# Weight-block sums of two seven-product multiplications: from VectorE and a table in HBM to accumulating DMAs at load time

## The chip, the core and the metric

The kernel runs on one NeuronCore of a Trainium2 chip. Its work is spread over TensorE (PE, with its weight loads PEld), VectorE (DVE), ScalarE (ACT), GpSimd (POOL) and the queue that issues most DMAs (SP). The metric is the device time of one execution in microseconds; lower is better.

## The reference, cut to what matters

The program is one block of a streaming encoder, in float32, for 16 meta tokens and 1024 frames of width 1024: a token mixer with four mLSTM heads and four retention heads, an output projection with a residual, and a gated MLP with a causal convolution, a down projection and a residual.

```
h = h + token_mixer(rmsnorm(h, norm_mix_g), ...)        # ends in: (mixed @ w_out)
h = h + channel_mixer(rmsnorm(h, norm_ffn_g), ...)
    a = causal_dwconv(u @ w_up, ffn_conv_w)
    (silu(a) * (u @ w_gate)) @ w_down
return rmsnorm(h, norm_final_g)
```

`w_out` is 2048 x 1024 and `w_down` 2816 x 1024. The change concerns these two products alone.

## The kernel before, in words

Every float32 matmul is made of three: both operands are split into a high and a low part (`hi`, rounded by ACT, and `lo`, the rest by DVE), and hi·hi, hi·lo and lo·hi are added up in PSUM.

The time runs in stages: the eight heads (token mixer), the output product `w`, the up and gate products, the down product `d`. In the mixers each head has its o projection beside its scan, then the next head's v projection, then its q and k projections (`qk_group`, three pieces of the tokens each).

The output and the down product are computed by seven block products instead of eight (class `Seven`, objects `mixw` and `down`). The weight matrix is cut in 2 x 2 blocks: w11 and w21 are the two column halves of the upper rows, w12 and w22 those of the lower rows. The activations are cut in two row halves and two token halves, A1, A2, B1, B2. Products "1", "2" and "4" each use a plain weight block. The pairs "65" and "73" use two sums of blocks each, in one 128 x 1024 tile per step. A product goes over `kn` row blocks of 128 (8 for `w`, 11 for `d`); the steps (stage, k) stand in the order 1, 65, 73, 4, 2 for `w` and 1, 2, 65, 73, 4 for `d`. A step of "65" or "73" issues 24 matmuls of 128x512, into the PSUM banks `pwx`, `pwy` (or `pdx`, `pdy`), which `give` adds to the residual when a stage has ended.

Each step has three parts. `load` brings the weight tile from HBM by a DMA on SP, into a ring: the tiles `raw_w` (two, of the general ring `raw`) and then `wdh` and `wdl` (two halves each) for `w`, four `rd` tiles for `d`. `prep` splits it (CAST on ACT into `hi_w` or `hi_d`, TENSOR_TENSOR on DVE into `lo_w` or `lo_d`; three such pairs in a ring), and splits the activations (`rsplit`). `mms` issues the matmuls. A tile of the load ring is free again when its `lo` has been made; the load for the step four uses later waits for that. `wdh` and `wdl` lie in memory that the mixers' pool `mix` gives back; the first load into them waits for the last instruction that uses that pool, and among those users are the activation tiles `wtk` and `wtq` of step 65, k=0.

The weight sums of "65" and "73" are made long before, in the mixers: `wsum(g, k)` is called three times per head, after pieces of the q and k projections of heads 1 to 7, until its 19 calls are done (8 for `w_out`, 11 for `w_down`). A call loads two 128 x 1024 row blocks (tiles named `wsw` or `wsd`), makes four additions on DVE and stores four 128 x 512 results in HBM tensors, also named `wsw` and `wsd`. `load` of the later stages then reads one 512 KB tile of these.

A scheduler that the framework brings sets the order of instructions on each engine; the engines run their queues in that order and wait on semaphores. A DMA waits on the queue that issues it, and holds up what stands behind it there.

Of the kernel before, what the change touches and what calls it, by code (L numbers as in the profile page):

```python
# [17 lines left out]
P = 128  # L18
# [12 lines left out]
HB = 4 * P  # L31
# [30 lines left out]
def body(ctx, tc, h_in, vecs, cst, mask_in, rot, w_v0, w_v, w_fm, w_out, w_up, w_gate, w_down, out):  # L62
# [121 lines left out]
    sums = {(g, st, k): dram.tile([P, 2 * HB], F32, name=f"ws{g}{st}_{k}") for g, n in (("w", 8), ("d", KD)) for st in ("65", "73") for k in range(n)}  # L184

    def wsum(g, k):
        src, n = (w_out, 8) if g == "w" else (w_down, KD)
        a, b = (accp.tile([P, 2 * HB], F32, tag=f"rr{i}", name=f"ws{g}{k}_{i}") for i in range(2))
# [3 lines left out]
        after(nc.vector.tensor_tensor(w22, w21, w22, ALU.add), last["qk"])  # L192
        nc.vector.tensor_tensor(w21, w21, w11, ALU.subtract)
# [5 lines left out]
    wsums = [(g, k) for g, n in (("w", 8), ("d", KD)) for k in range(n)]  # L199

    def u_m(h):
        for b in range(2):
# [352 lines left out]
            m.append(nc.tensor.matmul(pt, al, xh_, start=False, stop=last and k == n - 1, skip_group_check=True))  # L555
        return m[0], m[-1]

    def rsplit(x, tiles, late=False):
        hi, lo = (t[:, :x.shape[1]] for t in tiles)
        m = nc.scalar.copy(hi, x), V.tensor_tensor(lo, x, hi.bitcast(F32), ALU.subtract)  # L560
        if late:
            behind(m)
        else:
            last["rsplit"] = m
        return hi, lo
# [9 lines left out]
    class Seven:  # L575
# [10 lines left out]
        def load(self, t):  # L586
# [5 lines left out]
            if st in self.QUARTER:  # L592
                kb, mb = self.QUARTER[st]
                if k % 2 == 0:
                    n = min(2, self.kn - k)
                    x = self.raw(st, nm)
                    nc.sync.dma_start(x[:, :HB * n].rearrange("p (k j) -> p k j", j=HB),
                                      self.wd[k + kb * self.kn:k + kb * self.kn + n, :, mb * HB:(mb + 1) * HB].rearrange("k p j -> p k j"))
                    r["w"] = x[:, :HB * n]
            else:  # L600
                x = self.raw(st, nm)
                nc.sync.dma_start(x[:, :2 * HB], sums[self.nm, st, k])
                r["l"] = x[:, :2 * HB]
            self.draws[t] = r

        def pre4(self, t):
# [23 lines left out]
        def prep(self, t):  # L630
# [17 lines left out]
            elif st in self.QUARTER:  # L648
                if k % 2 == 0:
                    self.w = fsplit(nm, [d["w"]])  # L650
                r = rsplit(act[{"1": "A1", "2": "A2", "4": "A1"}[st], k], self.rt(st, k, 0))
                self.ops[t] = [(half_of(self.w, k % 2), r, "xy"[st == "2"])]
            elif st == "65":
                a1, a2, b2 = (act[q, k] for q in ("A1", "A2", "B2"))
# [6 lines left out]
            else:  # L661
                w = fsplit(nm, [d["l"]])
                r7 = rsplit(act["B1", k], self.rt(st, k, 0))
                r3 = rsplit(act["B2", k], self.rt(st, k, 1))
                self.ops[t] = [(half_of(w, 1), r7, "x"), (half_of(w, 0), r3, "y")]
            self.read(t)

# [322 lines left out]
    for h in range(8):  # L990
# [595 lines left out]
```

## Time and profile before

| what | value |
|---|---|
| median of 3 runs | 1552.53 us (1551.2 to 1552.64) |
| profiled execution, its span | 1551.5 us; its own time is not given apart from the span |
| busy: PE, PEld, DVE, ACT, POOL | 1518.8, 1395.5, 1124.2, 737.2, 2.4 us |
| bytes moved by DMA | 197.41 MB, 127 GB/s on average |
| HBM written | 49.32 MB |

The span is the time from the first to the last instruction; it lies 1.0 us below the median of the runs. A row of a view names the line in the kernel, the engine, the operation, what is written and read, the shapes, the count and the durations. SP's own waiting and issuing is written SPq. The view by stretches gives the busy time of each engine in a piece of the span, then the granted clock of TensorE (PEclk), the busy share of the 16 DMA engines, and GB/s. Tile names in the profile carry no numbers, so that all four halves of the ring read `wdh` or `wdl`.

### The profile page before, as it was taken

Reading aid. Unit: us, or ns where it says so; the run is one execution under the profiler, and the core shown is the slowest. Engines: PE = TensorE matmul, PEld = TensorE weight load, DVE = VectorE, ACT = ScalarE, POOL = GpSimd, SP = SyncE. Lnnn points to the kernel's source line nnn. Section 1 sums busy time; section 2 is a strip of 40 time slices with the busy share of each in tenths; the row PEclk is TensorE's granted clock in tenths of the full one; section 3 lists DMA queues with packets and bytes.
Section 4 is the critical chain, followed back from the end, with each engine's and each line's share of the span. In section 5 each row is a group of like instructions: output and inputs, shape, how many; then the busy total and the mean of one; then the engine's idle time right before and its main releaser. Section 6 shows DMA issues by size and latency. Waiting matters only on the chain.

```text
span 1551.5 us, 25426 instructions
## 1 busy us (share of the span) xinstructions
PE 1518.8 (98%) x9763; PEld 1395.5 (90%) x9763; DVE 1124.2 (72%) x2388; ACT 737.2 (48%) x1493; POOL 2.4 (0%) x12
## 2 busy tenths in 40 slices
PE   8999999999999999999999999999999999999997
PEld 8989999999989999998788998999999999888887
DVE  8757768696767767678867778666666666778657
ACT  7574655455243343436454455444444444434443
POOL 0000000000000000000000000000000000000000
PEclk9999999999999999999999999999999999999999
DMA  6125435263533525226542326332222224923313
GB/s 219 36 70 163 152 110 188 79 218 97 181 122 126 167 85 189 94 91 245 177 139 100 101 78 195 96 102 89 82 80 78 82 82 137 385 96 116 95 42 109
DMA packets 92441, 197.41 MB, mean 127 GB/s; under 512 B 9048, under 2 KB 31264, under 8 KB 92320
## 3 DMA queue, kind: packets, MB, share of 16 engines
q1 hardware_dynamic: 92176, 195.73, 38.2%
q8 instruction: 76, 1.25, 0.3%
q14 instruction: 45, 0.37, 0.1%
q10 hardware_dynamic: 144, 0.07, 0.0%
HBM read 146.44 MB, written 49.32 MB: 126 GB/s over the span
## 4 chain that ended last, share of the span: by engine, by line
PE 87%; DMA 5%; DVE 4%; ACT 2%; issue 1%; SPq 0%; DVEq 0%; ACTq 0%
PE pv L373 4%; PE pv L374 4%; PE pv L375 3%; PE po L385 3%; PE po L384 3%; PE po L383 3%; PE pdx L553 3%; PE pdx L555 3%; PE pdx L554 3%; PE pup_x L554 2%; PE pup_x L555 2%; PE pga_x L553 2%; PE pga_x L555 2%; PE pga_x L554 2%; PE pup_x L553 2%; DMA A<-scr 2%
## 5 line engine op out<-in xcount | busy, mean ns | idle before, releaser
L373 PE MATMUL pv<-hi_v,uh 128*128 128x256 f32 (+1 forms) x512 | 147.1, 288 | 6.1 <-DVE vl L349 1.9
L374 PE MATMUL pv<-lo_v,uh 128*128 128x256 f32 (+1 forms) x512 | 146.6, 287 | 0.0
L375 PE MATMUL pv<-hi_v,ul 128*128 128x256 f32 (+1 forms) x512 | 146.0, 286 | 0.0
L383 PE MATMUL po<-uh,hi_o 128*128 128x386 f32 (+2 forms) x384 | 125.7, 327 | 0.0
L384 PE MATMUL po<-ul,hi_o 128*128 128x386 f32 (+2 forms) x384 | 123.9, 323 | 0.0
L385 PE MATMUL po<-uh,lo_o 128*128 128x386 f32 (+2 forms) x384 | 123.6, 322 | 0.0
L373 PEld LDWEIGHTS pv<-hi_v,uh 128*128 128x128 f32 x512 | 97.8, 191 | 10.1 <-issue 2.9
L374 PEld LDWEIGHTS pv<-lo_v,uh 128*128 128x128 f32 x512 | 97.7, 191 | 0.6 <-DVE lo_v L150 0.5
L375 PEld LDWEIGHTS pv<-hi_v,ul 128*128 128x128 f32 x512 | 97.7, 191 | 0.1
L242 ACT CAST hi_up<-raw_up 128x512 fp32r<-128x512 f32 (+1 forms) x52 | 36.5, 719 | 108.2 <-PE pga_z L554 61.0
L383 PEld LDWEIGHTS po<-uh,hi_o 128*128 128x128 f32 x384 | 72.9, 190 | 0.2
L384 PEld LDWEIGHTS po<-ul,hi_o 128*128 128x128 f32 x384 | 72.8, 190 | 0.2
L385 PEld LDWEIGHTS po<-uh,lo_o 128*128 128x128 f32 x384 | 72.7, 189 | 0.1
L243 DVE TENSOR_TENSOR lo_ga<-fraw_ga,hi_ga 128x512 fp32r<-128x512 f32 (+1 forms) x52 | 41.8, 807 | 36.9 <-ACT hi_ga L242 36.8
L553 PE MATMUL pup_x<-uh_g,hi_up 128*128 128x256 f32 (+1 forms) x240 | 67.2, 282 | 1.2 <-ACT uh_g L1021 1.2
L554 PE MATMUL pup_x<-ul_g,hi_up 128*128 128x256 f32 (+1 forms) x240 | 67.4, 283 | 0.1
L243 DVE TENSOR_TENSOR lo_up<-raw_up,hi_up 128x512 fp32r<-128x512 f32 (+1 forms) x52 | 41.2, 809 | 35.1 <-ACT hi_up L242 34.3
L383 PE MATMUL pq<-uh,hi_q 128*128 128x400 f32 (+2 forms) x192 | 63.2, 329 | 3.1 <-DVE vl L349 1.9
L555 PE MATMUL pup_x<-uh_g,lo_up 128*128 128x256 f32 (+1 forms) x240 | 66.2, 282 | 0.0
L383 PE MATMUL pk<-uh,hi_k 128*128 128x400 f32 (+2 forms) x192 | 62.3, 324 | 0.5 <-DVE rq L404 0.5
L243 DVE TENSOR_TENSOR lo_d<-rd,hi_d 128x1024 fp32r<-128x1024 f32 (+1 forms) x34 | 37.7, 1112 | 34.0 <-ACT hi_d L242 34.0
L384 PE MATMUL pq<-ul,hi_q 128*128 128x400 f32 (+2 forms) x192 | 62.1, 324 | 0.0
(747 smaller groups left out, 4981.4 us busy)
## 6 DMA issues: line engine op xcount, KB each, us to landing
wsd<-w_down_d SPq DMA_DIRECT2D x22, 512.0 KB, 4.1
wsd<-wsd SPq DMA_DIRECT2D x44, 256.0 KB, 2.5
raw_up<-w_up_d SPq DMA_DIRECT2D x22, 512.0 KB, 3.7
fraw_ga<-w_gate_d SPq DMA_DIRECT2D x22, 512.0 KB, 3.6
acts<-cv SPq DMA_DIRECT2D x44, 256.0 KB, 2.0
rd<-wsd SPq DMA_DIRECT2D x22, 512.0 KB, 3.3
wsw<-w_out_d SPq DMA_DIRECT2D x16, 512.0 KB, 4.3
raw_o<-w_fm_d SPq DMA_DIRECT2D x16, 512.0 KB, 3.5
```

The costliest lines, as they stand in the source:

```text
L242: nc.scalar.copy(hi[:, o:o + n], x)
L243: nc.vector.tensor_tensor(lo[:, o:o + n], x, hi[:, o:o + n].bitcast(F32), ALU.subtract)
L373: nc.tensor.matmul(pv[:L, :nv], a, hi[:, o:o + nv], start=kb == 0, stop=False)
L374: nc.tensor.matmul(pv[:L, :nv], a, lo[:, o:o + nv], start=False, stop=False)
L375: nc.tensor.matmul(pv[:L, :nv], b, hi[:, o:o + nv], start=False, stop=kb == KB - 1)
L383: nc.tensor.matmul(pt[:, :n], a, uh[kb][:, t0:t1], start=kb == 0, stop=False)
L384: nc.tensor.matmul(pt[:, :n], a, ul[kb][:, t0:t1], start=False, stop=False)
L385: nc.tensor.matmul(pt[:, :n], b, uh[kb][:, t0:t1], start=False, stop=kb == KB - 1)
L553: m.append(nc.tensor.matmul(pt, ah, xh_, start=first and k == 0, stop=False, skip_group_check=True))
L554: nc.tensor.matmul(pt, ah, xl_, start=False, stop=False, skip_group_check=True)
L555: m.append(nc.tensor.matmul(pt, al, xh_, start=False, stop=last and k == n - 1, skip_group_check=True))
```

## The change

`wsum` and the HBM tensors `sums` are gone, with their calls in the head loop. `load` of "65" and "73" now makes the sums itself, in the load tile, with signs chosen so that every step is an addition. A plain DMA on SP brings w21 into both halves of the tile (the source is read twice). DMAs on GpSimd's queue with `accum_op=ALU.add` then add to it: for "65" w22 to both halves (512 KB) and w11 to the first (256 KB); for "73" w11 to both halves (512 KB), then w22 and then w12 to the first (256 KB each). Each of them writes bytes that the one before it has written, and so waits for that one to land. The signs are made up for by negating the activations of "1" and of B2 (`minus`), and by subtracting in `give`.

```
-    sums = {(g, st, k): dram.tile([P, 2 * HB], F32, name=f"ws{g}{st}_{k}") ...}
-    def wsum(g, k):
-        ...
-        nc.sync.dma_start(a, src[k])
-        nc.sync.dma_start(b, src[k + n])
-        w11, w21, w12, w22 = a[:, :HB], a[:, HB:], b[:, :HB], b[:, HB:]
-        after(nc.vector.tensor_tensor(w22, w21, w22, ALU.add), last["qk"])
-        nc.vector.tensor_tensor(w21, w21, w11, ALU.subtract)
-        nc.vector.tensor_tensor(w11, w22, w11, ALU.subtract)
-        nc.vector.tensor_tensor(w12, w12, w11, ALU.subtract)
-        for st, i, x in (("65", 0, w11), ("65", 1, w22), ("73", 0, w12), ("73", 1, w21)):
-            nc.sync.dma_start(sums[g, st, k][:, i * HB:(i + 1) * HB], x)
...
-    def rsplit(x, tiles, late=False):
+    def rsplit(x, tiles, late=False, minus=False):
         hi, lo = (t[:, :x.shape[1]] for t in tiles)
-        m = nc.scalar.copy(hi, x), V.tensor_tensor(lo, x, hi.bitcast(F32), ALU.subtract)
+        if minus:
+            m = nc.scalar.mul(hi, x, -1.0), V.scalar_tensor_tensor(lo, x, -1.0, hi.bitcast(F32), ALU.mult, ALU.subtract)
+        else:
+            m = nc.scalar.copy(hi, x), V.tensor_tensor(lo, x, hi.bitcast(F32), ALU.subtract)
...
             else:                                    # load, stages "65" and "73"
-                x = self.raw(st, nm)
-                nc.sync.dma_start(x[:, :2 * HB], sums[self.nm, st, k])
-                r["l"] = x[:, :2 * HB]
+                x = self.raw(st, nm)[:, :2 * HB].rearrange("p (i j) -> p i j", j=HB)
+                w = [self.wd[k + kb * self.kn, :, mb * HB:(mb + 1) * HB].rearrange("p (i j) -> p i j", i=1) for mb in range(2) for kb in range(2)]
+                w11, w12, w21, w22 = w
+                both = lambda v: v.to_broadcast([P, 2, HB])
+                nc.sync.dma_start(x, both(w21))
+                if st == "65":
+                    more = [(x, both(w22)), (x[:, 0:1], w11)]
+                else:
+                    more = [(x, both(w11)), (x[:, 0:1], w22), (x[:, 0:1], w12)]
+                for dst, src in more:
+                    nc.gpsimd.dma_start(dst, src, accum_op=ALU.add)
+                r["l"] = x.rearrange("p i j -> p (i j)")
...
-                    V.tensor_tensor(self.rs(j + j0, half), self.banks[b, j], self.rs(j + j0, half), ALU.add)
+                    x = self.rs(j + j0, half)
+                    V.tensor_tensor(x, x, self.banks[b, j], ALU.add if j0 or st == "2" else ALU.subtract)
...
-                if (kind, p) in (("q", 0), ("q", 2), ("k", 1)) and wsums:
-                    wsum(*wsums.pop(0))
```

Three places show how the order moves. First DVE at the start of the q projection of head 1, before the change; `rq1`, `cvq1` and `vl` are tiles of that projection and of the v projection before it, `wsw0_0` and `wsw0_1` the two blocks of the first `wsum` call.

```order
L404 TENSOR_TENSOR rq1_0_1805<-pq1_0_1780,Rb_111 128x400
L884 RECIPROCAL z0_1_1551<-z0_1_1551 128x3
L192 TENSOR_TENSOR wsw0_1_1815<-wsw0_0_1814,wsw0_1_1815 128x512
L407 TENSOR_SCALAR cvq1_0_1808<-rq1_0_1805,vec_72 128x400
L402 COPY rq1_1_1851<-rq1_0_1805 128x3
L885 SCALAR_TENSOR_TENSOR mv0_1_1395<-mv0_1_1395,z0_1_1551 128x3
L349 SCALAR_TENSOR_TENSOR vl_189<-pv1_7_1666,Rc_180,vh_188 128x256
L781 TENSOR_TENSOR S0_7l_1660<-C0_7_1657,S0_7h_1659 128x258
L193 TENSOR_TENSOR wsw0_0_1814<-wsw0_0_1814 128x512
```

Rows of this kind, 76 in all, are gone after the change, and the projection's own rows close up.

Second, the loads of the output product's ring. SP before, from the last `raw_w` load of "65" to the loads of "73" (`wsw65_4` is the stored sum of step 65, k=4; `wm` are two plain row blocks for two tail tokens, `raw_up` weights of the up product):

```order
L602 DMA raw_w65_3_9148<-wsw65_3_132 128x1024
L231 DMA raw_up0_0_10185<-w_up_d 128x1024
L602 DMA wdh_9200<-wsw65_4_133 128x1024
L602 DMA wdh_9200<-wsw65_5_134 128x1024
L176 DMA wm_9247<-w_out_d 128x1024 x2
L602 DMA wdl_9201<-wsw65_6_135 128x1024
L602 DMA wdl_9201<-wsw65_7_136 128x1024
```

SP and then GpSimd's queue after, for the same four steps 65, k=4 to 7:

```order
L591 DMA raw_w65_3_8888<-w_out_d 128x2x512
L591 DMA wdh_8942<-w_out_d 128x2x512 x2
L176 DMA wm_8993<-w_out_d 128x1024 x2
L591 DMA wdl_8943<-w_out_d 128x2x512 x2
L214 DMA raw_up0_0_9959<-w_up_d 128x1024
```

```order
L597 DMA raw_w65_3_8888<-w_out_d 128x2x512
L597 DMA raw_w65_3_8888<-w_out_d 128x512
L597 DMA wdh_8942<-w_out_d 128x2x512 x2
L597 DMA wdl_8943<-w_out_d 128x2x512 x2
L597 DMA wdh_8942<-w_out_d 128x512 x2
L597 DMA wdl_8943<-w_out_d 128x512 x2
```

GpSimd, which had no DMA before, now issues the large additions of all four steps ahead of the small addition that completes the first of them.

At the same place PE, where it first uses `hi_w` of step 65, k=4, before:

```order
L554 MATMUL pwx2_9061<-wr65_20_9262,hi_w65_2_9258 128x512
L555 MATMUL pwx2_9061<-wr65_20_9262,lo_w65_2_9259 128x512
L554 MATMUL pwx3_9065<-wr65_20_9262,hi_w65_2_9258 128x512
L555 MATMUL pwx3_9065<-wr65_20_9262,lo_w65_2_9259 128x512
L553 MATMUL pwy0_9231<-wr65_41_9328,hi_w65_4_9332 128x512
L553 MATMUL pwy1_9235<-wr65_41_9328,hi_w65_4_9332 128x512
```

and after:

```order
L538 MATMUL pwy1_8981<-rr1_8733,lo_w65_3_9044 128x512
L538 MATMUL pwy2_8985<-rr1_8733,lo_w65_3_9044 128x512
L538 MATMUL pwy3_8989<-rr1_8733,lo_w65_3_9044 128x512
L536 MATMUL pwx0_8789<-wr65_40_9086,hi_w65_4_9082 128x512
L537 MATMUL pwx0_8789<-wr65_40_9086,hi_w65_4_9082 128x512
```

Step k=4 began after step k=2 and was mixed with k=3; it now begins when all 24 matmuls of k=2 and all 24 of k=3 are issued.

Third is a pattern with no counterpart before: GpSimd's queue in stage "73" of the down product (each step has one row 128x2x512 and two rows 128x512).

```order
L597 DMA rd73_2_15446<-w_down_d 128x2x512
L597 DMA rd73_1_15407<-w_down_d 128x512
L597 DMA rd73_2_15446<-w_down_d 128x512
L597 DMA rd73_3_15483<-w_down_d 128x2x512
L597 DMA rd73_2_15446<-w_down_d 128x512
L597 DMA rd73_3_15483<-w_down_d 128x512
```

Between the two small additions of a step stands the large addition of the next, which waits for that step's plain load.

More of the change, by code (lines that the diff above doesn't have):

```diff
@@ L181, in last_two @@
                 nc.vector.tensor_scalar(acc[:, t], raw[:, :D], mm[:, k, t:t + 1], None, ALU.mult)
-    sums = {(g, st, k): dram.tile([P, 2 * HB], F32, name=f"ws{g}{st}_{k}") for g, n in (("w", 8), ("d", KD)) for st in ("65", "73") for k in range(n)}
-    def wsum(g, k):
-        src, n = (w_out, 8) if g == "w" else (w_down, KD)
-        a, b = (accp.tile([P, 2 * HB], F32, tag=f"rr{i}", name=f"ws{g}{k}_{i}") for i in range(2))
-        nc.sync.dma_start(a, src[k])
-        nc.sync.dma_start(b, src[k + n])
-        w11, w21, w12, w22 = a[:, :HB], a[:, HB:], b[:, :HB], b[:, HB:]
-        after(nc.vector.tensor_tensor(w22, w21, w22, ALU.add), last["qk"])
-        nc.vector.tensor_tensor(w21, w21, w11, ALU.subtract)
-        nc.vector.tensor_tensor(w11, w22, w11, ALU.subtract)
-        nc.vector.tensor_tensor(w12, w12, w11, ALU.subtract)
-        for st, i, x in (("65", 0, w11), ("65", 1, w22), ("73", 0, w12), ("73", 1, w21)):
-            nc.sync.dma_start(sums[g, st, k][:, i * HB:(i + 1) * HB], x)
-    wsums = [(g, k) for g, n in (("w", 8), ("d", KD)) for k in range(n)]
     def u_m(h):
```

4 lines of the change are left out of this document (2 added, 2 removed).

## The prediction

> **What bounds the kernel now.** I read the page's totals first, then the stretches, then the waits of PE in the mixers, and last the loads of the two stages that the change feeds.
>
> ```profile
> span 1551.5 us, 25426 instructions
> PE 1518.8 (98%) x9763; PEld 1395.5 (90%) x9763; DVE 1124.2 (72%) x2388; ACT 737.2 (48%) x1493; POOL 2.4 (0%) x12
> ```
>
> PE is busy 1518.8 of 1551.5 us. Whatever leaves PE's work alone can win at most the 32.7 us in which PE is idle, and can lose any time by which a weight tile comes late. The change leaves the matmuls as they are, so both sides are questions of waiting.
>
> ```profile
> 130.00:335.00 205.00, 200.06 (x1422) 194.44 (x1421) 155.86 (x428) 110.18 (x229) 0.00 (x0) 1.00 0.48 151
> 335.00:662.00 327.00, 322.87 (x2373) 315.18 (x2372) 235.95 (x586) 129.99 (x315) 0.00 (x0) 0.99 0.41 137
> 747.00:758.00 11.00, 11.00 (x49) 8.91 (x48) 10.46 (x15) 5.99 (x9) 0.00 (x0) 1.00 0.93 348
> 781.00:825.00 44.00, 44.00 (x191) 35.48 (x190) 31.66 (x44) 24.30 (x38) 0.00 (x0) 1.00 0.42 134
> 1386.00:1447.00 61.00, 61.00 (x265) 49.55 (x264) 49.58 (x71) 26.42 (x39) 0.00 (x0) 1.00 0.33 108
> 1447.00:1508.00 61.00, 61.00 (x265) 49.31 (x264) 32.08 (x45) 23.40 (x36) 0.00 (x0) 1.00 0.22 69
> ```
>
> The columns are the stretch, its length, busy PE, PEld, DVE, ACT and POOL, granted clock, DMA share and GB/s. The first two rows hold all 19 calls of `wsum`: PE is idle there 4.94 and 4.13 us, 9.1 in all. The last two are "65" and "73" of the down product: PE is never idle, a step lasts 61/11 = 5.55 us, and the DMA engines are two thirds free. The third row is the moment in the output product when the ring moves to `wdh` and `wdl`: there the DMA engines are 93% busy already, at 348 GB/s, which makes 348/0.93 = 374 GB/s when full. I use that rate below.
>
> **The part that goes: the sums in the mixers.**
>
> ```profile
> PE tr L896 <- DVE mx L903: 2.7, 3, 1.5
> PE n L818 <- ACT num L852: 2.4, 1, 2.4
> PE pq L383 <- DVE vl L349: 1.9, 2, 1.2
> PE n L818 <- ACT S_0h L780: 1.3, 1, 1.3
> PE pk L383 <- DVE rq L404: 0.5, 1, 0.5
> PE n L820 <- DVE pt_1l L781: 0.2, 1, 0.2
> L192 DVE TENSOR_TENSOR wsd<-wsd,wsd x11: 681/691/693, 339.2 to 655.6; 128x512 f32<-128x512 f32 x11
> L193 DVE TENSOR_TENSOR wsd<-wsd x11: 681/684/692, 340.2 to 656.7; 128x512 f32<-128x512 f32 x11
> wsd<-w_down_d SPq DMA_DIRECT2D x22, 512.0 KB, 4.1
> wsd<-wsd SPq DMA_DIRECT2D x44, 256.0 KB, 2.5
> rd<-wsd SPq DMA_DIRECT2D x22, 512.0 KB, 3.3
> ```
>
> The first six rows are all of PE's recorded waits between 130 and 662 us (total, times, longest); the next two are two of a call's four additions (min, median and max ns); the last three are DMAs with their size and their time to landing. Gone are 19 x 4 additions of 0.685 us, 52 us of DVE, and 38 loads and 76 stores, some 40 MB. DVE is busy 392 of these 532 us, and what it does beside PE costs nothing. Of PE's waits none is for a sum; 5.3 us (2.7 + 1.9 + 0.5 + 0.2) are for DVE instructions that may stand behind one, 3.7 for ACT. Ends: a gain of 9.1, if every idle moment vanishes, and a loss of 1, since the rows are packed anew. The sums stand in the q and k stage and most of the waits at its entry and in the scans, so I take a gain of 2.
>
> **The small edits.** 38 activation splits become SCALAR_TENSOR_TENSOR and a scaled copy.
>
> ```profile
> L560 DVE TENSOR_TENSOR rr<-wa,rr 128x512 fp32r<-128x512 f32 x28 | 19.1, 685 | 4.5 <-ACT rr L560 4.5
> L1263 DVE SCALAR_TENSOR_TENSOR cv<-s0up,vec,cv 128x512 f32<-128x512 f32 x20 | 15.0, 751 | 0.4
> ```
>
> That is 38 x 0.066 = 2.5 us of DVE, covered by PE, which is never idle in the down rows above; without that cover it would cost 2.5. `give` keeps its shape, with subtract in place of add. Both: 0.
>
> **The part that comes: 95 accumulating DMAs.** Per step they are one of 512 KB and one of 256 KB in "65", and one of 512 KB and two of 256 KB in "73", each behind the landing of the last. No transfer of this kind is in the trace. Lower end: a plain transfer of the size, 3.3 us for 512 KB and 2.5 for 256 KB by the rows above. For the value, I add one more passage of the bytes at the full rate, because the old bytes must be fetched too: 0.52 MB / 374 GB/s = 1.4, so 4.7 and 3.2 us, and twice the plain engine time. Upper end: three times the engine time (fetch, fetch back, store, none overlapped).
>
> The Trainium skill, DMA: Bandwidth & Descriptors, section "Anatomy of one DMA — SWDGE (gpsimd) path", gives about 2.0 us plus bytes at 436 GB/s for a DMA issued from GpSimd; as an estimate by that page, 3.2 and 2.6 us. By it the sum would be that of the cheap rival below. The skill's Collectives: The Full Stack, section "The bandwidth ceiling: the fold count and why AG ≠ RS ≠ AR", says that an add inside a DMA needs two source reads and so ran at about half the copy rate; it speaks against the change, and no run here shows it yet.
>
> *Output product, step 65, k=4.*
>
> ```profile
> 746.31 0.39 PE L555 MATMUL pwy<-wtq,lo_w 128*128 128x512 f32 x1
> 746.85 0.80 SPq L602 DMA_DIRECT2D wdh<-wsw  x2
> 747.69 0.90 SPq L176 DMA_DIRECT2D wm<-w_out_d  x2
> 748.93 1.03 SPq L602 DMA_DIRECT2D wdl<-wsw  x2
> DMA to landing us min/median/max: 8.0/8.0/8.0
> 750.75 1.05 ACT L242 CAST hi_w<-wdh 128x1024 fp32r<-128x1024 f32 x1 [2.15 <-DMA wdh<-wsw]
> 755.59 0.86 PE L553 MATMUL pwy<-wr,hi_w 128*128 128x512 f32 x3
> ```
>
> The start and the length stand first. The last matmul that reads `wtq` ends at 746.70; call it T0. The six loads start at T0 + 0.15, the last of them (second `wdl`, the landing row) lands 8.0 us after its issue, about T0 + 10.8; ACT already waits 2.15 us for the first. By the order, PE has 3 + 24 + 24 matmuls of 0.231 us (61 us for 265) after T0 before it needs k=4, so it needs it at T0 + 11.8. But the small addition that completes k=4 stands on GpSimd behind the large ones of k=4 to 7, and these behind the four loads. What passes before it lands is 6 loads (3.15 MB), four large additions at two passages (4.2 MB) and itself (0.5 MB): 7.85 MB / 374 = 21 us, and 1.05 for the cast: T0 + 22.1. PE waits 10.3 us. With additions at one passage it is 5.5 MB = 14.8, some 2 us for the last latency (3.3 less 1.4), 1.05: a wait of 6. At three, 10.2 MB = 27 us: 16.5. I take 10.
>
> *Output product, other steps.* For k=0 the chain is 3.2 + 4.7 + 3.2 from SP's issue:
>
> ```profile
> 719.54 13.14 SPq L602 DMA_DIRECT2D raw_w<-wsw  x4
> 734.47 0.40 PE L555 MATMUL pwx<-rr,lo_w 128*128 128x512 f32 x1
> 725.51 1.05 ACT L242 CAST hi_w<-raw_w 128x1024 fp32r<-128x1024 f32 x1
> ```
>
> It is split by 732 where 726.6 was; stage "1" keeps PE until 734.9 less the six matmuls that the order takes out of it, 733.5. The second ring buffer and k=2 and 3 come out about even. 0, with ends 0 and 5. In "73" (the row from 781 us, where PE is never idle) a step of 2.6 MB at two passages is 7 us against 5.5, 12 us over eight steps; but while PE waits at k=4, and through the four steps that follow it, the loads of "73" run on: 0, up to 8.
>
> *Down product.* SP issues a step's load when the tile four back has been split:
>
> ```profile
> 1379.48 31.09 SPq L602 DMA_DIRECT2D rd<-wsd  x7
> 1377.15 1.05 ACT L242 CAST hi_d<-rd 128x1024 fp32r<-128x1024 f32 x1 [1.95 <-PE pdy L554]
> 1396.62 1.05 ACT L242 CAST hi_d<-rd 128x1024 fp32r<-128x1024 f32 x1 [1.34 <-PE pdx L554]
> ```
>
> The load at 1379.48 goes into the tile whose cast began at 1377.15, and is itself cast four `rd` casts later, at 1396.62: 17.1 us, of which it now uses 3.3. With the additions a step of "65" needs 3.3 + 4.7 + 3.2 = 11.2 us, one of "73" 14.4, so latency alone is covered. The rate is not: "65" moves 0.52 + 2 x 0.79 = 2.1 MB, 5.6 us of the full engines, just a step; "73" moves 0.52 + 2 x 1.05 = 2.6 MB, 7.0 us against 5.55, 1.45 late each step, 16 in 11 steps, less the 2.7 to 4 us of cover: 12 us. At one passage it is 4.2 us a step, and 0. At three passages 9.8 us, 47 us late, and "65" adds 11 x 2.2 = 24: some 65.
>
> **Sum.** -2 + 0 + 10 + 0 + 12 = 20 us on the span of 1551.5; that is 1571.5, and 1 us more against the median: 1572.5, rounded to 1573.
>
> **The rivals.** *Cheap additions* (one passage): PE waits 6 us at k=4, none in the down product, 2 are gained: 1552.5 + 4 = 1556.5. For it speaks that the down loads land in 3.3 us on engines 33% busy; against it, that bytes must come from two places.
>
> *The additions bind* (three passages, or GpSimd's queue needs over 2 us for each): between two additions of a step the queue holds the next step's, so a step takes two landings and an issue; at 16 us at k=4 and 40 or more in the down product it is 1606 to 1635. For it speaks only that the upper ends are not excluded.
>
> *Faster*: the sums on DVE do hold up the mixers, all 9.1 us of PE's idle time there go, and k=4's additions are quick enough that PE waits less than that. It decides at a wait of 9 us; with cheap additions, 6 at k=4, the time is 1549.5. Against it: 3.7 of the 9.1 us are waits for ACT, and PE did not wait for a sum once.
>
> *Nothing to see*: 3.1 us either way is 0.2%, about what a measurement of this kernel can tell from no change; the cheap rival with 4 or 5 us gained in the mixers ends there.
>
> **Chances.** Forecast 0.46, cheap additions with a loss over 0.2% 0.16, additions bind 0.19, faster 0.11, nothing 0.08. Slower is 0.81 then. The range leaves out the far half of the binding rival and half of the faster one: 1551 to 1612. The forecast's own range, with 6 to 14 at k=4 and 2 to 25 down, is 1558 to 1592.
>
> **What would show it.** PE's waits in the mixers fall by about 2 us. Before k=4 of "65" ACT's cast of `wdh` waits for a DMA and PE then stands about 10 us. In the down product "65" stays near 61 us and "73" takes about 73, with casts waiting for DMAs on `rd`. DMA bytes stay near 197 MB and HBM writes fall by 20 MB. It is wrong if an accumulating 512 KB lands within 3.5 us (then nothing below) or beyond 6 (then "65" of the down product slows too), or if GpSimd takes over 2 us to issue one.

## The result and the profile after

The changed kernel takes 1687.26 us (median of 4 runs, 1681.73 to 1687.67) against 1552.59; the ratio is 1.0863, 95% interval 1.0846 to 1.0879. The forecast was 1573. The sign was right, the loss is 135 us in place of 20, and it lies beyond the whole range (1551 to 1612). Times of several runs, here and below, are medians of their fast ones; a single run can't be told to be fast or slow.

The page's totals of the changed kernel come first:

```profile
span 1685.3 us, 25366 instructions
PE 1558.1 (92%) x9763; PEld 1416.2 (84%) x9763; DVE 1087.6 (65%) x2312; ACT 733.5 (44%) x1491; POOL 99.9 (6%) x107
```

The matmuls are the same 9763, yet PE is busy 1558.1 us where it was 1518.8. So of 133.8 us more span, 94.5 are PE standing still longer and 39.3 are slower matmuls. The timeline of PE (start, length, engine, operation, and in brackets the idle time before and its releaser) cuts the run at the first matmul of the output product and of the down product, first in the old kernel and then in the new:

```profile
705.89 0.73 PE L553 MATMUL pwx<-rr,hi_w 128*128 128x512 f32 x2 [0.17 <-ACT rr L560]
1321.36 0.63 PE L553 MATMUL pdx<-uh_d,hi_d 128*128 128x512 f32 x2
```

```profile
692.51 0.72 PE L536 MATMUL pwx<-rr,hi_w 128*128 128x512 f32 x2 [1.00 <-ACT rr L544]
1391.10 0.63 PE L536 MATMUL pdx<-uh_d,hi_d 128*128 128x512 f32 x2
```

The mixers gain 13.4 us. From the first of these marks to the second it is 615.5 us before and 698.6 after: 83.1 lost. The up and gate products lie in this stretch, too, but take no longer than before. Their first matmul into `pup_x` starts at 926.0 and 997.3 us, which leaves 395.4 and 393.8 to the second mark (before, then after; duration min/median/max in ns, first and last start):

```profile
L553 PE MATMUL pup_x<-uh_g,hi_up x240: 276/282/386, 926.0 to 1298.5; 128*128 128x256 f32 x69, 128*128 128x258 f32 x51
L536 PE MATMUL pup_x<-uh_g,hi_up x240: 276/282/293, 997.3 to 1368.2; 128*128 128x256 f32 x69, 128*128 128x258 f32 x51
```

So the 83.1 us are lost in the output product. From the second mark to the end it is 230.1 and 294.2: 64.1 lost, in the down product. The table by stretches of the changed kernel (columns as in the prediction: length, busy PE, PEld, DVE, ACT, POOL, granted clock, DMA share, GB/s) shows the two mixer stretches, the middle of the output product, and "65" and "73" of the down product:

```profile
130.00:335.00 205.00, 204.44 (x1459) 199.60 (x1458) 150.85 (x414) 113.72 (x234) 0.00 (x0) 1.00 0.27 79
335.00:662.00 327.00, 327.00 (x2417) 321.70 (x2416) 217.56 (x552) 129.40 (x312) 0.00 (x0) 1.00 0.21 69
760.00:800.00 40.00, 21.21 (x77) 16.20 (x77) 17.35 (x20) 9.24 (x12) 8.45 (x8) 0.74 0.74 149
800.00:840.00 40.00, 23.91 (x82) 17.86 (x83) 18.56 (x27) 9.27 (x14) 12.88 (x13) 0.79 0.85 174
1455.30:1548.00 92.70, 73.06 (x266) 56.48 (x264) 47.14 (x66) 24.70 (x37) 25.35 (x24) 0.85 0.80 157
1548.00:1641.30 93.30, 71.12 (x265) 53.69 (x265) 35.62 (x51) 24.71 (x38) 25.66 (x26) 0.89 0.77 156
```

A step of "65" in the down product takes 92.70 / 11 = 8.43 us where it took 5.55, one of "73" 8.48. The DMA engines are 0.80 busy there at 157 GB/s, where the old kernel had 0.33 at 108. Per step of "65" that is 0.80 x 8.43 = 6.7 us of full engines for 1.32 MB, in place of 0.33 x 5.55 = 1.8 us for 0.60 MB: 3.7 times the work for 2.2 times the bytes. PE idles 19.6 us in "65", and the same 265 matmuls take 73 us in place of 61, at a granted clock of 0.85. The waits (total, times, longest) and the DMA queues and issues (size, count, median us to landing) name what is late:

```profile
ACT hi_d L225 <- DMA rd<-w_down_d: 103.9, 16, 9.8
POOL rd L597 <- DMA rd<-w_down_d: 101.8, 26, 8.3
PE pwx L536 <- ACT hi_w L225: 21.4, 2, 16.9
PE pwy L536 <- ACT wr L544: 12.4, 1, 12.4
PE pdy L536 <- ACT uh_d L546: 13.9, 3, 4.9
```

```profile
q1 hardware_dynamic: 80624, 155.87, 28.3%
q0 software_dynamic: 18544, 34.87, 12.8%
rd<-w_down_d POOLq DMA_DIRECT2D x22, 512.0 KB, 6.6
rd<-w_down_d POOLq DMA_DIRECT2D x33, 256.0 KB, 4.5
```

ACT's casts wait for the tiles, GpSimd (POOL) waits between its own additions, and PE waits for the casts or for activation splits (`wr`, `uh_d`), which ACT makes in the same queue. An addition of 512 KB lands in 6.6 us, one of 256 KB in 4.5. The queue q0 is the additions: 12.8% of 16 engines' 1685.3 us is 3451 us for 34.87 MB, 99 ns per KB; q1, the plain transfers, needs 28.3%, 49 ns per KB. A byte added costs twice the engine time of a byte copied. The Trainium skill, Collectives: The Full Stack, section "The bandwidth ceiling: the fold count and why AG ≠ RS ≠ AR", has an add read two sources and run at about half the copy rate. The two rows agree with the rate; whether a second read is the reason they don't show.

### The profile page after: what moved, and what is told of

The parts are those of the page before. It is cut to its first block, busy times and chain, and to the rows that moved or that the text cites. A ratio compares the mean times of both kernels' runs of the same rounds, so it can differ in the third digit from the quotient of the medians.

```text
span 1685.3 us, 25366 instructions
## 1 busy us (share of the span) xinstructions
PE 1558.1 (92%) x9763; PEld 1416.2 (84%) x9763; DVE 1087.6 (65%) x2312; ACT 733.5 (44%) x1491; POOL 99.9 (6%) x107
## 3 DMA queue, kind: packets, MB, share of 16 engines
q1 hardware_dynamic: 80624, 155.87, 28.3%
q0 software_dynamic: 18544, 34.87, 12.8%
## 4 chain that ended last, share of the span: by engine, by line
PE 76%; issue 9%; DMA 8%; POOL 3%; DVE 2%; ACT 1%; SPq 0%; POOLq 0%; DVEq 0%; ACTq 0%
PE pv L356 4%; PE po L366 3%; PE po L368 3%; PE po L367 3%; PE pv L357 3%; PE pv L358 3%; DMA wdh<-w_out_d 2%; PE pup_x L537 2%; PE pup_x L538 2%; PE pup_x L536 2%; PE pga_x L536 2%; PE pga_x L538 2%; PE pga_x L537 2%; POOL rd L597 2%; DMA rd<-w_down_d 2%
## 5 line engine op out<-in xcount | busy, mean ns | idle before, releaser
L597 POOL DMA_DIRECT2D rd<-w_down_d x55 | 56.5, 1081 | 693.4 <-DVE ul_d L546 562.1
L225 ACT CAST hi_d<-rd 128x1024 fp32r<-128x1024 f32 (+1 forms) x34 | 32.3, 958 | 139.1 <-DMA rd<-w_down_d 103.9
L536 PE MATMUL pdy<-uh_d,hi_d 128*128 128x512 f32 x132 | 54.7, 444 | 26.2 <-ACT uh_d L546 13.9
```

The lines of the kernel that those rows point to most:

```text
L225: nc.scalar.copy(hi[:, o:o + n], x)
L536: m.append(nc.tensor.matmul(pt, ah, xh_, start=first and k == 0, stop=False, skip_group_check=True))
L597: nc.gpsimd.dma_start(dst, src, accum_op=ALU.add)
```

## The experiments: what the additions cost

**No additions.** Below, B is the old kernel; an edit without a name is made to the changed one. The first run keeps the plain load and drops the rest.

```diff
-                for dst, src in more:
-                    nc.gpsimd.dma_start(dst, src, accum_op=ALU.add)
```

> No additions at all: each tile of "65" and "73" holds only what SP's plain load brings, so the sums are left out of the result. Theory M (what the mixers gain comes from what was taken out of them, whatever stands at the loads): the first matmul of the output product comes at about 692.5 us as in the changed kernel, 13.4 before the old kernel's 705.9, the output product up to the down product lasts 615.5 and the down product about 230 us as before, and the time is 1539. Rival (the load that writes one block twice is late by itself, or something else held the output product): the mixers gain the same, but PE waits at k=4 of "65" and the time is 1545 or more.

1541.8 us, 0.993 of before (0.9913 to 0.9946). From its timeline, the same two marks:

```profile
692.31 0.72 PE L536 MATMUL pwx<-rr,hi_w 128*128 128x512 f32 x2 [1.05 <-ACT rr L544]
1306.63 0.63 PE L536 MATMUL pdx<-uh_d,hi_d 128*128 128x512 f32 x2
```

The products are back to 614.3 us and, to the span's end at 1537.2, 230.6. So the additions cost 1687.3 - 1541.8 = 145 us, and removing the sums from the mixers gains 11 us (13.6 by the mark). Theory M holds; the rival does not.

**The same DMAs without the add, and the same adds with a quarter of the bytes.**

```diff
-                    nc.gpsimd.dma_start(dst, src, accum_op=ALU.add)
+                    nc.gpsimd.dma_start(dst, src)                                         # e2
+                    nc.gpsimd.dma_start(dst[:, :, :P], src[:, :, :P], accum_op=ALU.add)   # e3
```

> The same 95 DMAs in the same order on GpSimd's queue, each still behind the landing of the last, but as plain copies without the addition, so the tiles hold single blocks and not the sums. Theory of the addition (fetching the old bytes is what costs): a copy of 512 KB lands in about 3.6 us, a step of the down product's "65" takes 3.6 + 2.1 of issues = 5.7 us, near PE's 5.55, and the time is 1540 to 1560. Theory of the queue (GpSimd issues and lands slowly whatever it carries): steps stay at 7 us or more in the down product, PE waits again at k=4 to 7 of the output product, and the time is 1600 or more.

> The same 95 additions on the same queue and in the same chain, but each of a quarter of the columns, so the sums are made in a quarter of the tile only. Theory of bytes (an addition is slow by what it moves): with 6.0 us for 512 KB and 4.0 for 256 KB where little else runs, a line through the two gives 3.0 and 2.5 us for 128 and 64 KB; a step of "65" takes 3.0 + 2.1 of issues = 5.1 us, below PE's 5.55, the waits go and the time is 1540 to 1550. Rival (the number of additions, a fixed cost of each, binds): landings stay at 5 us or more, a step of "65" at 7 or more, and the time is above 1600.

1578.4 and 1580.6 us (one run each). Both kernels keep 95 DMAs on GpSimd's queue in the same chain, and both lose some 37 to 39 us against the run without; the other 107 to 109 us of the change come from adding whole tiles. First the queue, landings and the two down stretches of the copies, then the landings and stretches of the quarter additions:

```profile
q0 software_dynamic: 10032, 34.87, 6.6%
rd<-w_down_d POOLq DMA_DIRECT2D x22, 512.0 KB, 5.1
1399.50:1463.80 64.30, 62.20 (x266) 49.32 (x266) 45.55 (x64) 24.67 (x36) 15.12 (x24) 1.00 0.69 226
1463.80:1532.70 68.90, 64.38 (x266) 50.32 (x265) 35.86 (x51) 24.62 (x39) 14.34 (x24) 0.98 0.58 197
```

```profile
rd<-w_down_d POOLq DMA_DIRECT2D x22, 128.0 KB, 4.0
1408.10:1469.20 61.10, 61.10 (x266) 49.62 (x265) 49.69 (x70) 26.50 (x38) 26.60 (x26) 1.00 0.67 146
1469.20:1535.20 66.00, 62.85 (x266) 49.23 (x265) 31.64 (x46) 23.11 (x37) 21.99 (x22) 1.00 0.46 95
```

The copies take 6.6% of 16 engines for the same 34.87 MB, 48 ns per KB, half of the additions. In the two down stretches they lose 133.2 - 2 x 61 = 11 us, and the quarter additions 5; the clock stays at 0.98 or more. So there the bytes of the additions are what binds, not their number. The rest of the 37 to 39 us, 26 and 36 by the marks, lies in the output product. There a quarter of the bytes leaves 36 of 84 us, so bytes alone are not the cause. The wait before step k=4 of "65" shows it best. In the changed kernel it is 16.9 us, with plain copies of all the bytes 5.7, and with quarter additions still 14.0:

```profile
771.25 0.79 PE L536 MATMUL pwx<-wr,hi_w 128*128 128x512 f32 x1 [14.00 <-ACT hi_w L225]
```

In both runs four large additions stand on GpSimd's queue ahead of the small one that completes k=4. What GpSimd waits for between them, the profile doesn't name, so this part of the cause stays open. Both results miss both theories as I wrote them: no loss was expected from the one, 1600 or more from the other. A copy on this queue lands in 5.1 us here. The Trainium skill, DMA: Bandwidth & Descriptors, section "Anatomy of one DMA — SWDGE (gpsimd) path", gives 2.0 us plus bytes at 436 GB/s, as an estimate 3.2 us; beside the other traffic of this kernel (a DMA share of 0.69 and 0.58 in the rows above) the row doesn't agree, and the measurement decides.

**The order on GpSimd's queue.** The timeline of GpSimd in "65" shows what suggested it: the small addition of a step and the large one of the next are issued as a pair, then GpSimd stands until the large one lands.

```profile
1482.00 2.14 POOL L597 DMA_DIRECT2D rd<-w_down_d  x2 [6.27 <-DMA rd<-w_down_d]
1489.40 2.17 POOL L597 DMA_DIRECT2D rd<-w_down_d  x2 [5.27 <-DMA rd<-w_down_d]
```

The first run only writes the additions in another order:

```diff
-                for dst, src in more:
-                    nc.gpsimd.dma_start(dst, src, accum_op=ALU.add)
+                add = lambda m: nc.gpsimd.dma_start(*m.pop(0), accum_op=ALU.add)
+                big = add(more)
+                for u in sorted(self.pend):
+                    if self.pend[u]:
+                        add(self.pend[u])          # e9: after(add(self.pend[u]), big)
+                self.pend[t] = more
...
```

> The same additions of the same bytes, but on GpSimd's queue the small addition of a step stands behind the large one of the next step, and the second small one of "73" another step later. Theory of the queue's order (what binds is that the queue stands until the large addition has landed before it issues the small one and, with it, the next large one: 6.6 us plus 2.1 of issues a step): two additions are now in flight, a step of the down product takes what the DMA engines need, at most 0.80 x 92.7 / 11 = 6.7 us, its two stages with additions lose 25 us or less in place of 63, and the time is 1640 or less. Theory of the rate (the DMA engines, 0.80 and 0.77 busy in those stages, are in effect full): each landing grows as more of them overlap, the step stays at 8 us or more, and the time is within 10 us of 1687.

1682.9 us, but it tells nothing of the order in the down product: the scheduler, which rearranges what is written, put the queue there back into the pairs above. The second run forces the order.

> The same additions of the same bytes, with the order on GpSimd's queue set by force: the small addition of a step stands behind the large one of the next step, throughout both products. Theory of the queue's order (the pair of a step's small and the next step's large addition is issued only when the large one before has landed, so a step takes one landing of 6.6 us and 2.1 us of issues): two large additions are now in flight, a step of the down product falls to what the DMA engines need, 0.80 x 92.7 / 11 = 6.7 us, its two stages lose 25 us or less in place of 63, and the time is 1650 or less. Theory of the rate (the packets of the additions, 178 ns for 2 KB where a plain one takes 84, are what fills the engines): a landing takes longer as more additions overlap, the step stays at 8 us or more, and the time is within 15 us of 1687.

1686.7 us (one run, as is the one before), the time that the theory of the rate gave. Its stretches "65" and "73" of the down product:

```profile
1467.10:1546.30 79.20, 63.91 (x265) 50.07 (x264) 46.84 (x65) 24.62 (x37) 24.81 (x24) 0.95 0.92 192
1546.30:1641.10 94.80, 74.71 (x264) 57.20 (x265) 35.66 (x51) 24.86 (x39) 24.04 (x25) 0.82 0.72 144
```

In "65" the order does count, against that theory: a step falls from 8.43 to 7.20 us. But the engines are 0.92 busy then, and 0.92 x 7.20 = 6.6 us of engine time a step is what the pairs needed too (0.80 x 8.43 = 6.7). That is over PE's 5.55, so order alone would not bring the loss to zero. In "73" the deeper order helps nothing (8.62 us), and the output product is 11 us slower (692.90 to 1402.92 by its marks), which takes the gain back. In "65" the engine time sets the floor, and the chain of landings keeps the step above it. How the rest divides between the two in "73" stays open.

**Slower matmuls.** The matmuls behind PE's longest wait, in the changed kernel:

```profile
785.24 0.79 PE L536 MATMUL pwx<-wr,hi_w 128*128 128x512 f32 x1 [16.93 <-ACT hi_w L225]
787.11 0.63 PE L536 MATMUL pwx<-wr,hi_w 128*128 128x512 f32 x1
787.54 0.63 PE L537 MATMUL pwx<-wr,hi_w 128*128 128x512 f32 x1
788.49 0.40 PE L536 MATMUL pwy<-wr,hi_w 128*128 128x512 f32 x1
788.72 0.39 PE L537 MATMUL pwy<-wr,hi_w 128*128 128x512 f32 x1
```

These are five of the sixteen that follow the wait. For 2.7 us one starts every 0.43 us, then every 0.23: some six matmuls are 0.2 us late each. The Trainium skill, TensorE: Matmul & The Clock Gate, section "Part 1: The HAM clock gate (the 'warmup' mystery)", says that an idle window of about 3.4 us halves the clock until PE has been busy about as long; the rows agree with the halving; the slow stretch is 2.7 us here. "65" and "73" have 38 steps in the two products, so the 39.3 us of extra busy time come to 1.0 us a step, about one such restart each. They were not counted one by one. The granted clock goes with it: 0.74 to 0.89 in the stretches of these stages above, 1.00 in the mixers. That the slow matmuls are a consequence of the waits and not another cause is borne out by the run without additions, in which PE is busy 1514.9 us.

## The experiments: what the mixers gain, and where sums are cheap

**VectorE's additions or the traffic?** The first four runs split the 11 us.

```diff
 # e4: B; e4b also wraps both loads of a call in after(..., last["qk"])
-        after(nc.vector.tensor_tensor(w22, w21, w22, ALU.add), last["qk"])
-        nc.vector.tensor_tensor(w21, w21, w11, ALU.subtract)
-        nc.vector.tensor_tensor(w11, w22, w11, ALU.subtract)
-        nc.vector.tensor_tensor(w12, w12, w11, ALU.subtract)
 # e7: B with nc.gpsimd for nc.vector in these four lines
 # e5: the run without additions, with four such lines on a constant, at the old places
+        c = cs[:, 0:1].to_broadcast([P, HB])
+        after(nc.vector.tensor_tensor(w22, c, c, ALU.add), last["qk"])
...
```

> The old kernel with its loads and stores in the mixers, but without the four VectorE additions of each call; the sums are left out of the result. Theory V (VectorE's 52 us of additions, although it is busy 392 of 532 us, held up PE's 13.4 us): the first matmul of the output product comes at 692 to 694 us and the time is 1538 to 1542, the 0.993 of the run without additions. Theory T (the traffic of 40 MB or the 114 DMAs on SP's queue did it): it stays at 703 to 706 and the time at 1549 to 1553.

1557.9 us, 1.0033 (1.0015 to 1.005), and no answer: without the sums to wait for, loads and stores moved into the first 130 us, where the DMA share went from 0.32 to 0.84, and PE idled 13.5 us in the next 205 where it had idled 4.9. It was run again with the loads held at their old place:

> Once more the old kernel without the four VectorE additions of a call, now with the loads of each call held at their old place on SP's queue (without that, the run before had them moved to the first 130 us, where the DMA engines went to 0.84). The sums are left out of the result. Theory V: first matmul of the output product at 692 to 695, time 1539 to 1543. Theory S, in the part that a store stands behind its loads and not behind a sum: 698 to 702. Theory T (the 40 MB themselves): 703 to 706, time 1549 to 1553.

> The run without additions (e0), with the old four VectorE additions of each call put back at their places in the mixers, on constants and not on weights: VectorE's 52 us are there, the mixers' loads and stores of the sums are not. The sums are left out of the result. Theory V (VectorE's time held up PE's 13.4 us): the first matmul of the output product comes at 702 to 706 us and the time is 1549 to 1553. Theory S (SP's queue and its traffic: stores that wait for a sum hold the loads behind them): it stays at 692 to 694, and the time at 1539 to 1543.

Traffic alone: 1548.0 us, 0.9977 (0.9965 to 0.9988), first mark at 698.29. VectorE alone: 1549.2 us, 0.9989 (0.9978 to 1.0001), first mark at 702.43. The first mark is what theory S gave, the second what theory V gave (702 to 706), so neither holds by itself. Each half put back costs most of the 11 us (7 and 9, as 0.9977 and 0.9989 stand to 0.993), and both together 11. By the first mark it is 6.0 and 10.1 of 13.6. So they don't add up fully. Why they don't was not shown; the scheduler also places other instructions anew each time.

> The old kernel with the four additions of each call on GpSimd in place of VectorE, everything else as before. Theory V: VectorE is rid of the same 52 us, and GpSimd, busy 2.4 us of the span, has 532 us for 76 additions: even at 3 us each they fit, and the time is 1538 to 1543. Rival (GpSimd's additions slow VectorE's own work, or a call takes so long that its tiles hold up the next): VectorE's means of the same shapes rise, and the time is 1550 or more.

1561.4 us, 1.0073 (1.0046 to 1.01). Two groups of VectorE's instructions (count, busy us, mean ns) between 130 and 662 us, in the old kernel and then with the sums on GpSimd, and the totals of the latter:

```profile
L179 DVE SCALAR_TENSOR_TENSOR acc<-raw_m,mm,acc 128x1024 f32<-128x1024 f32 x22 | 27.3, 1280 | 0.1
L409 DVE SCALAR_TENSOR_TENSOR cvk<-rk,vec,cvk 128x400 f32<-128x400 f32 (+2 forms) x27 | 15.0, 574 | 0.0
```

```profile
L179 DVE SCALAR_TENSOR_TENSOR acc<-raw_m,mm,acc 128x1024 f32<-128x1024 f32 x22 | 33.6, 1565 | 0.1
L409 DVE SCALAR_TENSOR_TENSOR cvk<-rk,vec,cvk 128x400 f32<-128x400 f32 (+2 forms) x27 | 20.6, 767 | 0.3
PE 1520.7 (98%) x9763; PEld 1398.0 (90%) x9763; DVE 1126.5 (72%) x2312; ACT 732.3 (47%) x1489; POOL 118.4 (8%) x88
```

VectorE has 76 instructions less and is as busy as before, 1126.5 us: its own instructions with two inputs in SBUF go from 1280 to 1565 ns. The rival's first half is right. The Trainium skill, GPSIMD Engine Reference, section "1. Specifications", has GpSimd and VectorE share their SBUF interfaces, with contention for just such instructions; the rows agree.

**Additions by DMA, but early.** First in tiles of 256 KB in the mixers, one call at a time and in pairs, with loads, additions and stores on GpSimd's queue:

```diff
+        add = lambda x, y: nc.gpsimd.dma_start(x, y, accum_op=ALU.add)
+        put = lambda x, st, i: nc.gpsimd.dma_start(sums[g, st, k][:, i * HB:(i + 1) * HB], x)
+        after(nc.gpsimd.dma_start(a, w21), last["qk"])
+        nc.gpsimd.dma_start(b, w21)
+        add(a, w22)
+        add(b, w11)
+        put(a, "65", 1)
...
```

> The sums are made by accumulating DMAs as in the change, with its signs, but in the mixers, in tiles of 256 KB, and stored to a table that the two products load as in the old kernel. A call is two plain loads, four additions of 256 KB and four stores, all on GpSimd's queue: with 4.5 us for an addition and 2.5 for a load or a store some 25 us in a row, and there are 19 calls in 530 us. Theory V with early additions (additions do no harm where the DMA engines are 0.21 to 0.27 busy and PE does not wait for them): the first matmul of the output product comes at 692 to 694, PE does not wait at k=4, and the time is 1538 to 1543. Rival (the additions slow the mixers' own loads, or the last sums of w are late): 1548 or more.

> The early additions (e6) once more, two calls at a time, so that GpSimd's queue holds the steps of two chains side by side and is through before the output product (in e6 the 19 calls ran on to 724 us, and the output product's first split, which takes the same buffers, waited 26.0 us for the last stores). Theory: GpSimd's queue takes some 40 us for two calls, ten pairs are through by 500 us, PE waits in the mixers as little as in e6 (3.4 us between 130 and 662 where the old kernel has 9.1), nothing waits at the output product, and the time is 1541 to 1548. Rival (additions that overlap slow the mixers' own loads): PE waits there grow beyond 9 us and the time is 1552 or more.

1575.7 us, 1.0163 (1.0122 to 1.0204), and 1567.1 us, 1.0103 (1.0084 to 1.0123): both rivals. One at a time they ran on until PE, at the output product's first split, waited 26.0 us for buffers that the last stores still held; in pairs, with nothing that holds them back, they ran at once and kept the DMA engines 0.80 busy in the first 130 us and 0.76 in the next 205, where the mixers load. Then straight into HBM, held back by a small load that waits for a stored result:

```diff
+        both = lambda v: v.to_broadcast([P, 2, HB])
+        x, y = (sums[g, st, k].rearrange("p (i j) -> p i j", j=HB) for st in ("65", "73"))
+        add = lambda d, v: nc.gpsimd.dma_start(d, v, accum_op=ALU.add)
+        for f in (lambda: nc.gpsimd.dma_start(x, both(w21)), lambda: nc.gpsimd.dma_start(y, both(w21)),
+                  lambda: add(x, both(w22)), lambda: add(y, both(w11)), lambda: add(x[:, 0:1], w11),
+                  lambda: add(y[:, 0:1], w22), lambda: add(y[:, 0:1], w12)):
...
```

> The sums are made by the same kind of accumulating DMAs, with the signs of the change, but early and straight into the table in HBM, with no tile in SBUF and no VectorE work; the two products load them as the old kernel does. GpSimd's queue runs the 8 calls for w once the first head's output has been stored, and the 11 for d once the first up block has been stored. A call is two copies of 512 KB, two additions of 512 KB and three of 256 KB. Theory (an addition is harmless where PE does not wait for it): by the landings of the change, 5 + 5 + 6.6 + 6.6 + 3 x 4.5 = 37 us a call, w's sums are there by about 500 us and d's by about 1300, both in time; the mixers keep most of the gain, since their traffic is 8 calls in place of 19: first matmul of the output product at 694 to 699, no waits at k=4, time 1542 to 1549. Rival (additions into HBM take twice as long or fill the DMA engines): d's sums come after 1385, or the loads of the up and gate products wait, and the time is 1553 or more.

1552.9 us, 1.0008 (0.9991 to 1.0024), and the first mark at 708.75: the theory missed both of its ranges, and it is the mixers that lose. The first stretch below holds w's 8 calls, the second most of d's 11:

```profile
130.00:335.00 205.00, 196.33 (x1398) 190.94 (x1397) 139.74 (x394) 110.51 (x231) 44.61 (x51) 0.99 0.80 177
1000.00:1330.00 330.00, 330.00 (x2074) 297.80 (x2073) 219.50 (x343) 143.89 (x260) 52.91 (x61) 1.00 0.72 179
```

Additions of the same kind go with 8.7 idle us of PE in the mixers (4.9 in the old kernel, 0.6 in the changed one) and none beside the up and gate products, at nearly the same DMA share. Two last runs: w's calls spread over the heads, and w's calls by VectorE as before (spread too), with d's in HBM.

> The early additions into HBM (e12) once more, but w's 8 calls are spread: each waits on GpSimd's queue for a store of a head's result, two calls behind the first head, one behind each of the next six. Theory of density (in e12 the 8 calls kept the DMA engines 0.80 busy from 130 to 335 us, and the mixers' own loads waited): the share stays near 0.5, PE idles 2 to 4 us between 130 and 662 in place of 11.3, the first matmul of the output product comes at 695 to 699 in place of 708.75, and the time is 1541 to 1546. Rival (any such traffic beside the mixers costs by its bytes): 705 to 709, and 1550 to 1554.

> The 8 sums of w made by VectorE in the mixers as in the old kernel, two calls in the second head's q part and one in each of the next six; the 11 of d by additions into HBM behind the mixers, as in e12, where they cost PE nothing. Theory of number (VectorE's additions and their traffic cost the mixers by the call): 8 of 19 calls leave 11 x 8/19 = 4.6 us of the 11 us that lie between the old kernel and the run without additions, first matmul at 697 to 699, time 1543 to 1547. Rival (a call or two at a bad place costs it): 703 or later, 1549 or more, or all of it goes, 692 to 694 and 1540 to 1542.

1546.9 us, 0.9976 (0.9961 to 0.999), and 1543.9 us, 0.9955 (0.9938 to 0.9971). The mixers' first stretch of both:

```profile
130.00:335.00 205.00, 202.06 (x1441) 196.79 (x1440) 148.12 (x406) 111.23 (x230) 23.11 (x27) 1.00 0.55 130
```

```profile
130.00:335.00 205.00, 203.69 (x1448) 199.06 (x1447) 154.84 (x425) 114.53 (x237) 0.00 (x0) 0.99 0.37 117
```

Spread, w's additions keep the share at 0.55, and PE idles 2.9 us there where it idled 8.7: the theory of density holds (first mark 695.9; its 1541 to 1546 is just missed by the median). The second run is within what the theory of number gave, 1543 to 1547 with the first mark at 697.3, and it beats both kernels, the old one by 0.5%: the sums of w as in the old kernel, those of d by accumulating DMAs into HBM while PE is busy with the up and gate products.

## Why the prediction was wrong

- *The sign, the place, the doubling*: right. The loss comes from additions landing late in both products; the engine time of an added byte is twice that of a copied one (99 against 48 ns per KB), as taken; HBM writes fall by 20 MB (49.3 to 29.4).
- *"So 4.7 and 3.2 us"*: 6.6 and 4.5, beyond the 6 us that the prediction named as its own end. It was priced as one DMA alone. In the products two are in flight beside the plain loads; how much of the difference that makes was not separated.
- *"5.6 us of the full engines, just a step"*: the failed step of the down product. Measured are 6.7 us of engine time a step, and 8.43 us a step. "65" was forecast to stand just at the bound and lost 32 us; "73" lost 32 in place of 16 less cover. Sum: 64 in place of 12, which was the upper end of the term (65). The term is mis-sized by its rate: 374 GB/s for full engines came from one stretch of 11 us. The row of the queue in the old kernel's page gives less: 38.2% of 16 engines' 1551.5 us for 195.73 MB is 48 ns per KB, 330 GB/s for all 16, and 2.1 MB at that rate are 6.4 us, already over 5.55.

```profile
q1 hardware_dynamic: 92176, 195.73, 38.2%
```

- *"so latency alone is covered"*: the second failed step of the down product. The step was checked against one tile's chain, but GpSimd's queue takes the steps one after another, a landing of 6.6 us and a pair of issues of 2.1, which is 8.7 against the 8.43 measured. So the engines reach 0.80 and not 1.00; with the order forced they reach 0.92 in "65". The rival of binding additions had this ("between two additions of a step the queue holds the next step's"), at 0.19, but its 1606 to 1635 priced no wait in the output product after k=4.
- *"It is split by 732 ... 0, with ends 0 and 5"*: a failed step of the output product. PE already waits before k=4, for 8.0 us at k=0 and 4.5 at k=3 alone:

```profile
729.54 0.80 PE L536 MATMUL pwy<-wtq,hi_w 128*128 128x512 f32 x1 [7.97 <-ACT hi_w L225]
761.12 0.80 PE L536 MATMUL pwx<-rr,hi_w 128*128 128x512 f32 x1 [4.49 <-ACT hi_w L225]
744.65 0.96 SPq L591 DMA_DIRECT2D wdh<-w_out_d  x2
784.14 1.04 ACT L225 CAST hi_w<-wdh 128x1024 fp32r<-128x1024 f32 x1 [12.54 <-DMA wdh<-w_out_d]
786.47 3.27 SPq L591 DMA_DIRECT2D wdh<-w_out_d  x2
```

- *"PE waits 10.3 us"* at k=4: 16.9, near the upper end (16.5), but by luck. The loads start at 744.65 and the tile of k=4 is cast by 785.2, 40.5 us later, where the prediction has 22. PE, late itself, comes to k=4 at 768.3, 23.7 us after them in place of 11.7. The two errors offset each other. Nor is it the bytes over the rate of the engines: by that sum quarter additions (4.3 MB in all) leave a wait of about 1 us, and 14.0 were measured.
- *"while PE waits at k=4 ... the loads of "73" run on"*: the other failed step there. No load of "73" starts during that wait; SP's next one is at 786.47, behind the split of k=4, which frees its tile. All four tiles of the ring hold unfinished steps until then. "73" then took 10.4 us a step in place of 5.6. By a count of PE's matmuls against the run without additions, about 22 us of the loss lie before k=4, 20 in k=4 to 7, and 39 in "73" (0, up to 8, in the prediction).
- *The matmuls were taken to keep their 0.231 us*: they don't behind a wait. 39 of the 134 us are that, and no term stood for it.
- *"I take a gain of 2" in the mixers*: 13.4 at the mark. That DVE's work beside PE costs nothing was wrong: the 52 us of additions, put back alone, cost 9 of the 11 us. The upper end given, 9.1, was the idle time between 130 and 662, and 8.5 of it did go (0.56 and 0.00 left), though none of the recorded waits was for a sum. A wait put down to another DVE or ACT instruction may go when what delays that one goes; this is argued and not shown. The other 5 us lie before 130 and after 662 and in the clock (0.98 became 0.99 before 130 us, and 0.99 became 1.00 from 335 to 662); they were not split further.

## What to carry to other kernels

Price an accumulating DMA at twice the engine time of a copy, count the whole chain of landings of a tile and the queue that issues it, and don't divide bytes by the rate of the best stretch; where the result stands close to the bound, expect it to lose. A sum that PE doesn't wait for can be made by such DMAs beside a stage with idle DMA engines, straight into HBM, if something holds them back from crowding an earlier stage. After each long wait, add the slow restart of the matmuls to the wait itself.

## What the hardware showed that I had not expected

- An addition goes out in more packets than a copy of the same bytes: 18544 against 10032 for 34.87 MB. That is not what doubles its price. In the packet records of the changed kernel's trace a 2 KB packet of an addition took 178 ns (median) and a plain 2 KB packet 84; the same DMAs without the add went out in 4 KB packets of 159 ns.
- GpSimd needs longer to issue an addition, too: in the run with early additions the rows of its queue read 0.89 us for an addition and 0.56 for a plain store.

```profile
641.45 0.89 POOL L190 DMA_DIRECT2D wsd<-w_down_d  x1 [2.15 <-DMA wsd<-wsd]
645.75 0.56 POOL L191 DMA_DIRECT2D wsd<-wsd  x1 [3.42 <-DMA wsd<-w_down_d]
```

- Additions on GpSimd make VectorE's own instructions with two SBUF inputs up to a third slower (574 to 767 ns), so that moving work off VectorE left it as busy as before.
